# First stage of an encoder layer: an earlier norm, another order of VectorE work and of projection units

## The chip, the cores and the metric

The kernel runs on one core of one Trainium2 chip. The metric is the device time of one execution in microseconds, the median of several runs of the same program. The core has a matrix engine (TensorE, PE in the profile; its weight loads are PEld), VectorE (DVE), ScalarE (ACT), GpSimd (POOL) and a queue of DMA issues (SP). Each engine takes its own instructions in program order and waits on semaphores for the others.

## The reference, cut to what matters

One layer over 1040 tokens (16 meta tokens and 1024 others) of width 1024, all in float32:

```
h = rmsnorm(x)
q, k, v, z, b, a, sc_b, sc_c, sc_x, gate_a, gate_b = split(h @ w_in)
o  = bidirectional chunked gated DeltaNet(silu(conv5(q, k, v)), b, a)     # 8 heads of 128
o  = rmsnorm(o) * silu(z)
ya = o @ w_branch_dn
yb = (sc_b * conv3(sc_c * sc_x)) @ w_branch_sc
x += (sigmoid(gate_a) * ya + sigmoid(gate_b) * yb) @ w_out
x += (silu(gate) * up) @ w_down,  gate, up = split(rmsnorm(x) @ w_gate_up)
out = rmsnorm(x)
```

Inside a head, per chunk of keys k and queries q with decay `exp(g_i - g_j)`: the triangular matrix `I + beta * (k k^T) * decay` is inverted, and a scan over chunks carries a 128x128 state S, forwards and backwards. The change touches the order in which these pieces are issued, not what is computed.

## The kernel before

The kernel has three stages: the projections together with the DeltaNet heads (the first stage, up to about 1060 us), then the branch projections, the merge and the output projection, then the gated feed-forward. Every large product is made as three products of split operands (high times high, high times low, low times high).

**Units.** The first stage is a list of units of projection work, each one column block of 128 of `w_in`. A unit is run by `dense_steps` (L333, matmuls at L340), 24 matmuls for each of its blocks of 320 to 512 tokens, which go into one of two PSUM banks (tag "m"). There are 24 units for q, k and v of the 8 heads (`u_qkv`, L374), 24 units of the short convolution branch (`u_short`, L421: C, X and B for each of 8 column blocks), 16 gate units (`u_gate`, L454) and 5 units of z (`u_z`, L463; the other three z blocks open the second stage, L1395). `pick` (L956) takes the next q, k or v unit when `qkv_ok` allows it and otherwise the first of `fill_units`, whose order before the change is: 24 short convolution units, 16 gate units, 5 z-units. `pick` also starts the load of the unit's weights on SP (L966), one unit ahead; `split_part` (L969) splits them into high and low halves, on ScalarE (L976) and VectorE (L973).

**What the units leave.** A q, k or v chunk is copied by ScalarE into a row buffer `ra` (two of them, `row_buffer`, L347) and convolved on VectorE over two halves (`conv_job`, L355; operations at L362 and L370). A short convolution unit fills a row buffer from C and X (L433, L436), `short_job` (L406; L410, L415) convolves it, B is multiplied in (L450), and the product is stored to `p_d` in device memory (L452). A gate unit is a tanh on ScalarE and a store (L459, L461). A z-unit is a tanh, a VectorE multiplication and a store (L473, L477, L479). The second stage begins with the last three z blocks, then loads all eight `p_d` (L1409) and splits them into `px` (tag "b", L100 and L101), on which the first branch product (L133 to L135) runs.

**Streams.** Beside the units, four streams work for the heads, each one head at a time: `g_decay` (L532) loads and masks the decay matrix PQ (mask at L540, exponential at L545), `g_norm` (L549) makes the chunk products, `g_inv` (L637) the inverse, `g_scan` (L769) the scan. They are Python generators that issue a few instructions and yield the time at which they want to go on. After every projection matmul, `run_streams` (L998) steps each stream that is due, in the order scan, inverse, norm, decay, and `pump` (L316) fills VectorE from three lanes of small jobs: convolutions ("conv"), the forward substitution of the inverse ("fs", L495 and L499) and small norms.

**The planner's clock.** The order is written out by hand, that is, no instruction is moved afterwards (`manual_schedule`). A model of the time stands behind it: `T` holds a time in ns for each engine, `pe(ns)`, `V(n, kind)` and `A(n)` (L265 to L277) advance it by the price of an instruction and return when its result is seen elsewhere. `pump` works while VectorE's modelled time is at most 700 ns ahead of PE's.

**The norm.** `g_norm` transposes k and q into PSUM (`tok`, banks of tag "e", three of them, L575 and its neighbours), takes squares on ScalarE (L563), and then loops over 8 chunks. `kkq(c)` (L602) multiplies a chunk's k with k and q into an "e" bank; two L625 operations make NP, one L629 operation makes PQ, both on VectorE. Before the change `kkq(c + 2)` is issued right after the L629 of chunk c, and the loop yields after the L625 pair and after L629, so other VectorE jobs get in between. `g_inv` begins with four VectorE transposes (L653) and ends with L764 and L765.

**What starts when.** `start_streams` (L979) starts a norm for head h when its convolutions are done and `h < done + 2`. `done` counts scans that have ended wholly, with their output norm (L912 to L920), transposes and stores (L935, L937); `freed` is raised inside the last of a scan's eight steps (L901), after its last L887 product. `g_decay` goes by `freed` already. In a scan step, L850 and L853 multiply the state, L860 forms the right side on VectorE, L866 applies the inverse, L883 and L887 follow, and L896 makes the new state on VectorE. NP has two buffers, and the scan of head h writes its output into NP of head h.

Of the kernel before, what the change touches and what calls it, by code (L numbers as in the profile page):

```python
# [8 lines left out]
F32 = mybir.dt.float32  # L9
# [7 lines left out]
P = 128  # L17
# [7 lines left out]
H = 8  # L25
# [22 lines left out]
def encoder_layer(ctx: ExitStack, tc: tile.TileContext, x, meta, norm1_w, w_in, w_ba,  # L48
# [15 lines left out]
    def uid(s):  # L64
        cnt["n"] += 1
        return f"{s}_{cnt['n']}"
# [198 lines left out]
    def on(e, ns, ready=0.0):  # L265

        T[e] = max(T[e], ready, T["pe"]) + ns
        return T[e] + TOPE
# [5 lines left out]
    def V(n, kind=0):  # L274
        return on("dve", (68 + 1.042 * n, 130 + 1.042 * n, 130 + 0.52 * n)[kind])
# [187 lines left out]
    def u_z(h, w):  # L463

        rest = None
        for i in range(2):
            po = psm()
            for k, _ in enumerate(dense_steps(po, w, hx, META + 512 * i, 512)):
                if k == 11 and rest:
                    rest()  # L470
                yield
            th = half_buffer()[:, :512]
            nc.scalar.activation(th, po, AF.Tanh, scale=0.5)  # L473
            A(512)

            def rest(i=i, th=th, po=po):
                nc.vector.scalar_tensor_tensor(out=th, in0=th, scalar=1.0, in1=po, op0=ALU.add, op1=ALU.mult)  # L477
                V(512)
                nc.sync.dma_start(z_d[h][:, 512 * i:512 * i + 512], th)  # L479
        T["dve"] = max(T["dve"], T["act"] + HOP)  # L480
        rest()
# [67 lines left out]
    def g_norm(h, st_):  # L549

        kq = st_["kq"]
        kT, qT = kq[:, 0], kq[:, 1]
        small = dn.tile([P, 9, 12], F32, tag="small", name=uid("small"), bufs=2)
        st_["small"] = small
        ssk, ssq, rk2, ssk1, y, tmp, sk = (small[:, :, i] for i in range(7))
        cc, ce = small[:, :, 7:9], small[:, :, 9:11]
# [43 lines left out]
        def kkq(c):  # L600
            pk = psd()
            mm(pk[:, :2 * P].rearrange("p (a t) -> p a t", a=2), kT[:, cs(c)], kq[:, :, cs(c)],  # L602
                                  start=True, stop=True)
            return pk, pe(435)

        nxt = [kkq(0), kkq(1)]
        yield T["act"] + HOP
        nc.vector.tensor_scalar(out=ssk1, in0=ssk, scalar1=EPS, scalar2=None, op0=ALU.add)
        nc.vector.reciprocal(rk2, ssk1)
# [2 lines left out]
        nc.vector.tensor_tensor(out=cc, in0=hb, in1=rk2.unsqueeze(2).broadcast_to([P, 9, 2]), op=ALU.mult)  # L612
        nc.vector.tensor_scalar(out=Nm, in0=Nm, scalar1=cc[:META, 8, 0:1], scalar2=None, op0=ALU.mult)
        on("dve", 500)
        NP = dn.tile([P, NC, 2, P], F32, tag="NP", name=uid("NP"), bufs=2)
        PQ = st_["PQ"]
        st_["NP"] = NP
        yield T["act"] + HOP - 300
        for c in range(NC):
            pk, t = nxt.pop(0)  # L620
            while c not in st_["exp"]:
                yield T["pe"] + 200
            yield max(t, st_["exp"][c])
            for d in range(2):
                nc.vector.scalar_tensor_tensor(out=NP[:, c, d], in0=pk[:, 0:P], scalar=cc[:, c, d:d + 1],  # L625
                                               in1=PQ[:, c, d], op0=ALU.mult, op1=ALU.mult)
                V(P, 1)
            yield T["dve"] - 200
            nc.vector.tensor_tensor(out=PQ[:, c], in0=pk[:, P:2 * P].unsqueeze(1).broadcast_to([P, 2, P]), in1=PQ[:, c],  # L629
                                    op=ALU.mult)  # L630
            V(2 * P)
            if c + 2 < NC:
                nxt.append(kkq(c + 2))
            yield T["dve"] - 200
        enqueue("norm", norm_job(st_, ssk1, cc, ce, he, y, tmp, sk))

    def g_inv(h, st_):  # L637
# [14 lines left out]
        for b in range(4):  # L652
            nc.vector.transpose(NP[B(b), :, 1, B(b)], NP[B(b), :, 1, B(b)])  # L653
            on("dve", 467)
            nc.sync.dma_start(nd[b].rearrange("c d j i -> j (c d) i"),
                                             NP[B(b), :, :, B(b)].rearrange("j c d i -> j (c d) i"))
            if b < 3:
                yield T["dve"] - 200
        nc.gpsimd.memset(fP, 0.0)
        nc.gpsimd.memset(fPf[0:64, 0:8 * 33:33], 1.0)  # L660
        nc.gpsimd.memset(fPf[0:64, 8 * 32 + 24:512:33], 1.0)
# [107 lines left out]
    def g_scan(h, st_):  # L769
# [159 lines left out]
        for c4 in range(2):  # L929
            oT = NP[:, 4 * c4:4 * c4 + 4, 1 - c4]  # L930
            pt = newbank()
            for c in range(4):
# [10 lines left out]
                 for h in range(H) for i, off in enumerate((OK, OQ, OV))]  # L943
    fill_units = [(off + j * P, lambda w, j=j, i=i: u_short(j, i, w), None, i)
                  for j in range(8) for i, off in enumerate((OSC, OSX, OSB))]
    fill_units += [(off + j * P, lambda w, j=j, d_=d_[j]: u_gate(j, d_, w), None, None)
                   for j in range(8) for off, d_ in ((OGA, ta_d), (OGB, tb_d))]
    fill_units += [(OZ + h * P, lambda w, h=h: u_z(h, w), None, None) for h in range(ZH)]
    done = freed = 0
    decs, norms, invs, scans = [], [], [], []  # L950

# [27 lines left out]
    def start_streams():  # L979
        nonlocal ndec, nnorm, ninv, nscan  # L980
        h = ndec
        if h < H and h < freed + 2 and not decs:
            decs.append([g_decay(h, heads[h]), T["dve"] + HOP, h])
            ndec += 1
        h = nnorm
        if h < H and h < ndec and h < done + 2 and not norms and all(k in heads[h] and heads[h][k]() for k in ("tk", "tq")):
            norms.append([g_norm(h, heads[h]), T["dve"] + HOP, h])
            nnorm += 1
        h = ninv
        if h < H and not invs and heads[h].get("normed"):  # L990
            invs.append([g_inv(h, heads[h]), T["dve"] + HOP, h])
            ninv += 1
        h = nscan
        if h < H and not scans and heads[h].get("inverted") and "tv" in heads[h] and heads[h]["tv"]():
            scans.append([g_scan(h, heads[h]), T["dve"] + HOP, h])
            nscan += 1
# [809 lines left out]
```

## Time and profile before

| | us |
|---|---|
| median of 3 runs (2005.18 to 2007.22) | 2005.81 |
| the profiled execution | 2006.06 |
| its span, first to last instruction | 2004.3 |
| PE busy in the span | 1985.3 (99%) |
| weight loads busy | 1730.0 (86%) |
| VectorE busy | 1334.7 (67%) |
| ScalarE busy | 816.9 (41%) |
| GpSimd busy | 116.5 (6%) |

In all rows of the profile, "<-" reads "waits for" in a list of waits and "out <- in" in a list of instructions; "x3" is a count; "idle before" is time in which the engine did nothing ahead of an instruction. Times in a timeline count from the first instruction of the span. A matmul's length is modelled and overlaps the next one; the distance between two starts is its cost. VectorE and ScalarE rows that follow each other overlap a little in the same way.

### The profile page before, as it was taken

The page shows a single profiled execution, that of the slowest core. Times are in us where ns is not written, and L with a number is a line of the kernel's source. Part 1 is how long each engine was busy: PE and PEld are TensorE (multiplying, and loading weights), DVE is VectorE, ACT ScalarE, POOL GpSimd, SP SyncE. Part 2 cuts the span into 40 slices and gives each one's busy share as a digit, 9 for nine tenths or more (in the row PEclk, how much of TensorE's full clock was granted, in tenths as well). Part 3 has the DMA queues.
Part 4 walks back from the last instruction along what each step waited for, and adds up shares of the span by engine and source line. Part 5 has one row for each costly group of instructions (what it writes and reads, how often), then busy time and mean ns, then how long its engine had stood idle before and what let it go on. Part 6 is the DMA issues. An engine that isn't in the chain of part 4 may idle for free.

```text
span 2004.3 us, 31913 instructions
## 1 busy us (share of the span) xinstructions
PE 1985.3 (99%) x12059; PEld 1730.0 (86%) x12059; DVE 1334.7 (67%) x2966; ACT 816.9 (41%) x1945; POOL 116.5 (6%) x407
## 2 busy tenths in 40 slices
PE   9999999999999999999999999999999999999998
PEld 8999999999899989888888888887878888888887
DVE  6888677879688878673325434468866666646575
ACT  6471353466255555543324111224423333334344
POOL 2002201002010202010000000000000000000000
PEclk9999999999999999999999999999999999999999
DMA  3121231302212231323237543123666345487654
GB/s 137 61 80 59 64 96 48 96 24 89 75 59 64 69 89 55 106 64 101 79 111 246 205 137 105 63 85 110 248 216 222 139 149 188 158 272 243 195 172 168
DMA packets 131409, 247.85 MB, mean 124 GB/s; under 512 B 45045, under 2 KB 54694, under 8 KB 128823
## 3 DMA queue, kind: packets, MB, share of 16 engines
q1 hardware_dynamic: 130679, 244.77, 36.9%
q8 instruction: 94, 1.54, 0.3%
q10 hardware_dynamic: 576, 1.05, 0.1%
q14 instruction: 60, 0.49, 0.1%
HBM read 179.10 MB, written 66.67 MB: 123 GB/s over the span
## 4 chain that ended last, share of the span: by engine, by line
PE 68%; DVE 5%; DMA 1%; ACT 1%; issue 1%; SPq 0%; DVEq 0%; ACTq 0%
PE pm L340 19%; PE pd L1546 10%; PE pe L1546 4%; PE pm L1546 3%; PE pe L133 1%; PE pe L134 1%; PE pe L135 1%; PE pd L133 1%; PE pd L135 1%; PE pd L134 1%; PE pe L1713 1%; PE pe L1712 1%; PE pe L1714 1%; PE pd L1713 1%; PE pd L1712 1%; PE pd L1714 1%
## 5 line engine op out<-in xcount | busy, mean ns | idle before, releaser
L340 PE MATMUL pm<-al,wh 128*128 128x512 f32 (+4 forms) x1424 | 495.9, 353 | 0.0
L340 PE MATMUL pm<-hTh,wh 128*128 128x512 f32 (+4 forms) x1424 | 495.0, 352 | 0.4 <-ACT hTh L1086 0.2
L340 PE MATMUL pm<-hTh,wl 128*128 128x512 f32 (+4 forms) x1424 | 495.1, 352 | 0.0
L340 PEld LDWEIGHTS pm<-al,wh 128*128 128x128 f32 x1424 | 266.9, 188 | 18.1 <-issue 1.1
L340 PEld LDWEIGHTS pm<-hTh,wh 128*128 128x128 f32 x1424 | 266.8, 188 | 18.0 <-ACT hTh L1086 0.8
L340 PEld LDWEIGHTS pm<-hTh,wl 128*128 128x128 f32 x1424 | 266.9, 188 | 16.7 <-issue 0.4
L973 DVE TENSOR_TENSOR wl<-raw,wh 128x512 fp32r<-128x512 f32 x134 | 90.4, 688 | 64.5 <-ACT wh L976 64.0
L101 DVE TENSOR_TENSOR al<-raw,ring_h 128x1024 fp32r<-128x1024 f32 x73 | 88.7, 1222 | 65.4 <-ACT ring_h L100 64.9
L100 ACT CAST ring_h<-raw 128x1024 fp32r<-128x1024 f32 x73 | 76.7, 1053 | 106.9 <-PE pe L1714 37.2
L362 DVE SCALAR_TENSOR_TENSOR kq<-ra,wc,kq 128x520 f32<-128x520 f32 x128 | 96.9, 757 | 5.8 <-ACT kq L392 4.3
L976 ACT CAST wh<-raw 128x512 fp32r<-128x512 f32 x134 | 79.1, 621 | 13.3 <-PE pm L340 9.6
L100 ACT CAST wh<-raw 128x1024 fp32r<-128x1024 f32 x43 | 45.1, 1050 | 87.8 <-PE pe L134 34.8
L495 DVE TENSOR_TENSOR tm<-fP,fN 128x135 f32<-128x135 f32 (+23 forms) x248 | 72.7, 293 | 6.6 <-DMA fN<-nd 2.5
L499 DVE TENSOR_TENSOR fP<-fP,tm 128x135 f32<-128x135 f32 (+23 forms) x248 | 71.6, 289 | 4.4
L873 ACT ACTIVATE w<-pd,small 128x128 f32<-128x128 f32 x128 | 39.9, 364 | 82.6 <-PE pd L866 75.3
L1649 ACT ACTIVATE b<-b 128x512 f32<-128x512 f32 x22 | 13.9, 632 | 115.4 <-DVE b L1548 115.4
L1548 DVE TENSOR_TENSOR b<-pd,b 128x512 f32<-128x512 f32 x22 | 15.2, 690 | 67.6 <-PE pd L1546 67.6
L101 DVE TENSOR_TENSOR wl<-raw,wh 128x1024 fp32r<-128x1024 f32 x43 | 52.4, 1219 | 11.6 <-ACT wh L100 11.4
L1546 PE MATMUL pd<-b_hl,wh 128*128 128x512 f32 x176 | 54.4, 390 | 0.0
L860 DVE SCALAR_TENSOR_TENSOR r<-pd,negEG,vS 128x128 f32<-128x128 f32 x120 | 36.7, 345 | 26.5 <-PE pd L850 26.5
L545 ACT ACTIVATE PQ<-PQ,negG 128x128 f32<-128x128 f32 x128 | 43.4, 395 | 24.3 <-DVE PQ L540 24.1
L840 ACT ACTIVATE jk<-NP 128x128 f32<-128x128 f32 x64 | 19.9, 311 | 81.8 <-DVE NP L836 80.8
(523 smaller groups left out, 4422.8 us busy)
## 6 DMA issues: line engine op xcount, KB each, us to landing
raw<-in_w_in_dram SPq DMA_DIRECT2D x72, 512.0 KB
raw<-in_w_gate_up_dram SPq DMA_DIRECT2D x44, 512.0 KB
sums<-in_w_down_dram SPq DMA_DIRECT2D x22, 512.0 KB
t_d<-sums SPq DMA_DIRECT2D x11, 1024.0 KB
raw<-s_d SPq DMA_DIRECT2D x44, 256.0 KB
raw<-t_d SPq DMA_DIRECT2D x44, 256.0 KB
act_d<-b SPq DMA_DIRECT2D x43, 256.0 KB
raw<-act_d SPq DMA_DIRECT2D x33, 256.0 KB
```

The source lines that it names most:

```text
L100: nc.scalar.copy(hi, src)
L101: nc.vector.tensor_tensor(out=lo, in0=src, in1=hi.bitcast(F32), op=ALU.subtract)
L133: mm(po[:m, :n], wh[:, k, :m], xhk[:, t0:t0 + n], start=(k == 0), stop=False)
L134: mm(po[:m, :n], wh[:, k, :m], xlk[:, t0:t0 + n], start=False, stop=False)
L340: mm(po[:, :n], ww[:, k], f(k)[:, t0:t0 + n], start=i == 0, stop=i == 3 * KT - 1)
L362: nc.vector.scalar_tensor_tensor(out=acc, in0=raw[:, h0 + t:h0 + t + hn], scalar=wc[:, t, col:col + 1], in1=acc, op0=ALU.mult, op1=ALU.add)
L495: nc.vector.tensor_tensor(out=tv, in0=fP[:, 0:r, j:j + 1].broadcast_to([P, r, n]), in1=fN[:, j:j + 1, j + 1:32].broadcast_to([P, r, n]), o ...
L499: nc.vector.tensor_tensor(out=fP[:, 0:r, j + 1:32], in0=fP[:, 0:r, j + 1:32], in1=tv, op=ALU.subtract)
L545: nc.scalar.activation(PQ[:, c, d], PQ[:, c, d], AF.Exp, bias=negG2[:, c, hd:hd + 1])
L973: nc.vector.tensor_tensor(out=u[1][1][:, k], in0=u[2][:, k], in1=u[1][0][:, k].bitcast(F32), op=ALU.subtract)
L976: nc.scalar.copy(u[1][0][:, k], u[2][:, k])
L1546: mm(po, x[:, k], y, start=k + i == 0 and not add_to, stop=k == 3 and i == 2, skip_group_check=add_to)
```

## The change

A norm may start when `h < freed + 2`. It holds before it takes its NP buffer until `h <= done + 1`. Since a norm can now begin while the scan two heads back still uses its `small` tile, `small` has three buffers instead of two.

In the loop over chunks, `ask()` issues `kkq` when the model says that the bank it will use is free (`freed_at`) and fewer than two are waiting. The two L625 and the L629 of a chunk are issued together, and the loop goes on when PE's modelled time is within 800 ns of the end of what VectorE has been given. As `pump` stops at 700 ns, lanes get little in between. The yield between the first transposes of `g_inv` goes from 200 ns to 800 ns ahead of VectorE.

`fill_units` is turned round: gate units, z-units, and the 24 short convolution units at the end.

```diff
--- before.py
+++ after.py
@@ -550,7 +550,7 @@
 
         kq = st_["kq"]
         kT, qT = kq[:, 0], kq[:, 1]
-        small = dn.tile([P, 9, 12], F32, tag="small", name=uid("small"), bufs=2)
+        small = dn.tile([P, 9, 12], F32, tag="small", name=uid("small"), bufs=3)
         st_["small"] = small
         ssk, ssq, rk2, ssk1, y, tmp, sk = (small[:, :, i] for i in range(7))
         cc, ce = small[:, :, 7:9], small[:, :, 9:11]
@@ -603,7 +603,14 @@
                                   start=True, stop=True)
             return pk, pe(435)
 
-        nxt = [kkq(0), kkq(1)]
+        nxt, freed_at, asked = [kkq(0), kkq(1)], [0.0], 2
+
+        def ask():
+
+            nonlocal asked
+            while asked < NC and asked < len(freed_at) + 2 and freed_at[asked - 2] <= T["pe"]:
+                nxt.append(kkq(asked))
+                asked += 1
         yield T["act"] + HOP
         nc.vector.tensor_scalar(out=ssk1, in0=ssk, scalar1=EPS, scalar2=None, op0=ALU.add)
         nc.vector.reciprocal(rk2, ssk1)
@@ -612,26 +619,33 @@
         nc.vector.tensor_tensor(out=cc, in0=hb, in1=rk2.unsqueeze(2).broadcast_to([P, 9, 2]), op=ALU.mult)
         nc.vector.tensor_scalar(out=Nm, in0=Nm, scalar1=cc[:META, 8, 0:1], scalar2=None, op0=ALU.mult)
         on("dve", 500)
+        while h > done + 1:
+            yield T["pe"] + 100
         NP = dn.tile([P, NC, 2, P], F32, tag="NP", name=uid("NP"), bufs=2)
         PQ = st_["PQ"]
         st_["NP"] = NP
         yield T["act"] + HOP - 300
+        freed_at[0] = T["act"] + HOP
         for c in range(NC):
+            while not nxt or c not in st_["exp"]:
+                ask()
+                yield T["pe"] + 100
             pk, t = nxt.pop(0)
-            while c not in st_["exp"]:
-                yield T["pe"] + 200
-            yield max(t, st_["exp"][c])
+            while T["pe"] < max(t, st_["exp"][c]):
+                ask()
+                yield T["pe"] + 100
             for d in range(2):
                 nc.vector.scalar_tensor_tensor(out=NP[:, c, d], in0=pk[:, 0:P], scalar=cc[:, c, d:d + 1],
                                                in1=PQ[:, c, d], op0=ALU.mult, op1=ALU.mult)
                 V(P, 1)
-            yield T["dve"] - 200
             nc.vector.tensor_tensor(out=PQ[:, c], in0=pk[:, P:2 * P].unsqueeze(1).broadcast_to([P, 2, P]), in1=PQ[:, c],
                                     op=ALU.mult)
-            V(2 * P)
-            if c + 2 < NC:
-                nxt.append(kkq(c + 2))
-            yield T["dve"] - 200
+            freed_at.append(V(2 * P))
+            ask()
+            ready = T["dve"] - 800
+            while T["pe"] < ready:
+                yield T["pe"] + 100
+                ask()
         enqueue("norm", norm_job(st_, ssk1, cc, ce, he, y, tmp, sk))
 
     def g_inv(h, st_):
@@ -655,7 +669,7 @@
             nc.sync.dma_start(nd[b].rearrange("c d j i -> j (c d) i"),
                                              NP[B(b), :, :, B(b)].rearrange("j c d i -> j (c d) i"))
             if b < 3:
-                yield T["dve"] - 200
+                yield T["dve"] - 800
         nc.gpsimd.memset(fP, 0.0)
         nc.gpsimd.memset(fPf[0:64, 0:8 * 33:33], 1.0)
         nc.gpsimd.memset(fPf[0:64, 8 * 32 + 24:512:33], 1.0)
@@ -946,6 +960,7 @@
     fill_units += [(off + j * P, lambda w, j=j, d_=d_[j]: u_gate(j, d_, w), None, None)
                    for j in range(8) for off, d_ in ((OGA, ta_d), (OGB, tb_d))]
     fill_units += [(OZ + h * P, lambda w, h=h: u_z(h, w), None, None) for h in range(ZH)]
+    fill_units = fill_units[24:] + fill_units[:24]
     done = freed = 0
     decs, norms, invs, scans = [], [], [], []
 
@@ -983,7 +998,7 @@
             decs.append([g_decay(h, heads[h]), T["dve"] + HOP, h])
             ndec += 1
         h = nnorm
-        if h < H and h < ndec and h < done + 2 and not norms and all(k in heads[h] and heads[h][k]() for k in ("tk", "tq")):
+        if h < H and h < ndec and h < freed + 2 and not norms and all(k in heads[h] and heads[h][k]() for k in ("tk", "tq")):
             norms.append([g_norm(h, heads[h]), T["dve"] + HOP, h])
             nnorm += 1
         h = ninv
```

## The prediction

> **What bounds the kernel now.** I read the windows first, five of 200 us over the first stage and one behind it. Their columns are length, busy time of PE, weight loads (PEld), DVE, ACT and POOL, then granted clock, DMA share and GB/s.
>
> ```profile
> 50.00:250.00 200.00, 199.84 (x1433) 189.29 (x1432) 161.29 (x399) 86.42 (x269) 26.28 (x99) 1.00 0.21 66
> 250.00:450.00 200.00, 199.40 (x1694) 188.40 (x1693) 158.65 (x457) 103.42 (x341) 14.08 (x61) 1.00 0.22 66
> 450.00:650.00 200.00, 199.24 (x1647) 186.23 (x1647) 163.01 (x483) 94.30 (x311) 27.02 (x91) 1.00 0.23 71
> 650.00:850.00 200.00, 199.02 (x1591) 178.94 (x1590) 155.00 (x469) 107.69 (x345) 28.33 (x90) 1.00 0.26 79
> 850.00:1050.00 200.00, 199.88 (x1243) 168.16 (x1242) 85.64 (x276) 69.32 (x191) 8.95 (x32) 1.00 0.28 87
> 1050.00:1250.00 200.00, 200.00 (x884) 165.60 (x883) 92.28 (x100) 48.89 (x52) 0.00 (x0) 1.00 0.53 177
> ```
>
> In the five rows of the first stage PE idles 0.16 + 0.60 + 0.76 + 0.98 + 0.12 = 2.62 us of 1000. VectorE, the engine that the change reorders, is 78 to 82% busy up to 850 us and 43% behind it. The clock is full in every row. So the order can only be worth what PE waits, unless the order changes what PE's work itself costs. That second point I read from PE's timeline: the scan of the last head between projection matmuls.
>
> ```profile
> 941.10 0.40 PE L340 MATMUL pm<-al,wh 128*128 128x512 f32 x1
> 941.33 0.60 PE L866 MATMUL pd<-r,NP 128*128 128x128 f32 x4
> ...
> 942.01 0.39 PE L340 MATMUL pm<-hTh,wh 128*128 128x512 f32 x1
> 942.24 0.39 PE L340 MATMUL pm<-al,wh 128*128 128x512 f32 x1
> ...
> 944.77 0.40 PE L340 MATMUL pm<-hTh,wl 128*128 128x512 f32 x1
> 945.00 0.61 PE L850 MATMUL pd<-S,kq 128*128 128x128 f32 x4
> 945.45 0.61 PE L853 MATMUL pd<-S,kq 128*128 128x128 f32 x4
> ...
> 946.13 0.40 PE L340 MATMUL pm<-al,wh 128*128 128x512 f32 x1
> ```
>
> The second column (0.40) is a matmul's modelled length; the work is the distance of starts, 942.24 − 942.01 = 0.23 for a projection matmul. One small group costs 942.01 − 941.10 − 2 × 0.23 = 0.45 us. Two groups side by side cost 946.13 − 944.77 − 2 × 0.23 = 0.90, which is twice 0.45. Going in and out of a group is thus not charged extra, and whichever step stands between whichever projection matmuls, the sum is the same. A reordering moves this work and removes none.
>
> [...]
>
> What PE waits for in the first stage (35 to 1050 us; total, times, longest), first the matmuls' own rows and then those of their weight loads:
>
> ```profile
> PE pd L850 <- DVE S L896: 0.8, 2, 0.6
> PE pe L602 <- DVE PQ L629: 0.7, 1, 0.7
> PE pd L754 <- DVE XT L746: 0.4, 1, 0.4
> ...
> PEld pd L850 <- DVE S L896: 2.6, 6, 0.9
> ...
> PEld pe L602 <- PE pm L340: 1.1, 1, 1.1
> ...
> PEld pe L602 <- PE pd L97: 0.3, 1, 0.3
> ```
>
> Lateness of VectorE in the loads' rows is 2.6 at the scan's states and 1.1 + 0.3 at the norm's products; with the 0.4 of L754 it makes 4.4 us. These are the terms that this change can reach.
>
> **The change part by part. 1, asking for kkq only when its bank is free.** The 0.7 looks like this on PE and on VectorE:
>
> ```profile
> 503.91 0.40 PE L340 MATMUL pm<-hTh,wl 128*128 128x512 f32 x1
> 505.01 0.67 PE L602 MATMUL pe<-kq 128*128 128x256 f32 x2 [0.71 <-DVE PQ L629]
> ...
> 503.11 0.60 DVE L625 SCALAR_TENSOR_TENSOR NP<-pe,small,PQ 128x128 f32<-128x128 f32 x2
> 503.63 0.24 DVE L499 TENSOR_TENSOR fP<-fP,tm 128x96 f32<-128x96 f32 x1
> 503.79 0.74 DVE L415 SCALAR_TENSOR_TENSOR rb<-ra,cols,rb 128x512 f32<-128x512 f32 x1
> 504.45 0.41 DVE L629 TENSOR_TENSOR PQ<-pe,PQ 128x256 f32<-128x256 f32 x1
> ```
>
> L602 was issued although its PSUM bank waits for L629, and L629 stood behind a short convolution and a step of the inverse (503.63 to 504.45). Every projection matmul queued behind L602 waited too: 1.10 − 0.23 = 0.87 us. The new loop asks by the modelled time at which the bank is free. Bounds: 0 (the model is late by as much as now) and 1.4 (both rows). I take 0.9, the one stall whose rows show it. The number of products stays, and so do the two L625 and one L629 of a chunk.
>
> **2, precedence of the decay loop.** Chunks now follow each other: two L625 take 0.52 from start to start and L629 0.34 (timeline at 639.85 to 640.19 below), so 8 chunks hold VectorE 8 × 0.86 = 6.9 us in which scan operations, convolutions and the inverse get only the gaps.
>
> ```profile
> 636.25 0.69 DVE L765 COPY NP<-pd 64x512 f32<-64x512 f32 x1 [1.84 <-ACT NP L764]
> ...
> 639.85 0.42 DVE L629 TENSOR_TENSOR PQ<-pe,PQ 128x256 f32<-128x256 f32 x1
> 640.19 0.60 DVE L625 SCALAR_TENSOR_TENSOR NP<-pe,small,PQ 128x128 f32<-128x128 f32 x2
> ...
> 646.24 0.42 DVE L653 STREAM_TRANSPOSE NP<-NP 32x256 f32<-32x256 f32 x1
> ```
>
> The planner books these operations, so a scan matmul is placed later and PE runs projections instead: 0, hidden by the projections. Without that cover each chunk that delays a state costs 0.86.
>
> **3, the norm two heads back starts at `freed`, not `done`.** What is skipped is the tail of a scan. For the last head the rows are:
>
> ```profile
> 976.62 0.61 PE L887 MATMUL pd<-v,PQ 128*128 128x128 f32 x4
> ...
> 984.99 1.26 ACT L935 COPY NP<-pd 128x512 f32<-128x512 f32 x2 [4.60 <-PE pd L97]
> ```
>
> That is 986.25 − 976.62 = 9.6 us here. The transposes and squares move into it; the loop waits for `done`, since NP has two buffers. But a head's inverse is one at a time: L765 ends the previous one at 636.94 and L653 begins the next at 646.24. The head gains at most those 9.3 us in this place. What is late next is the inverse, not PE. Earlier heads shorten the stage only if projections run out, and they do not:
>
> ```profile
> 1059.58 0.32 SPq L479 DMA_DIRECT2D z_d<-rb  x1
> 1063.51 7.87 SPq L1409 DMA_DIRECT2D s<-p_d  x5
> 1073.93 2.59 SPq L1409 DMA_DIRECT2D s<-p_d  x3
> ...
> 1084.29 1.22 DVE L101 TENSOR_TENSOR b<-s,b 128x1024 fp32r<-128x1024 f32 x1
> ...
> 1089.31 0.39 PE L133 MATMUL pd<-b,wh 128*128 128x512 f32 x1
> ```
>
> The last z-unit of the stage is stored from 1059.58, so projections run on for some 73 us past the last head's end at 986.25. Worth 0. The third `small` buffer costs no instruction.
>
> **4, short convolutions last.** Their VectorE work up to now lies among the heads:
>
> ```profile
> L415 DVE SCALAR_TENSOR_TENSOR rb<-ra,cols,rb 128x512 f32<-128x512 f32 x32 | 23.9, 745 | 0.3
> L450 DVE TENSOR_TENSOR rb<-pm,rb 128x512 f32<-128x512 f32 x16 | 10.9, 683 | 2.1 <-PE pm L340 2.0
> ```
>
> With the smaller operations of the same units left out these are 34.8 us, part of which moves to where VectorE is 43% busy. Over the four busy rows, 637.95 us of VectorE, that is some 5%, so the lateness at L850 (2.6 us in 6 stalls) shrinks and does not vanish, the more so as heads come closer together. Bounds 0 and 2.6; between ends this far apart I take 1.1, just under the half, since convolutions of q, k and v stay among the heads. Moved with it: 16 stores to p_d, which now come last on SP's queue, past the gates' and z-units' stores. The loads at L1409 follow them. Now the first load waits from 1059.58 to 1063.51 behind a z-store; then it waits behind a p_d store of the same size. The eighth load is issued by 1076.52, 17 us after the last store. Its result is split by 1085.51 and PE wants it 7 × 3 × 0.23 = 4.8 us after 1089.31, so 8.6 us are spare: 0, and only what exceeds 8.6 if that cover is gone.
>
> **5, the inverse's yield of 800 instead of 200.** It puts up to three transposes earlier on VectorE: 0, hidden by the inverse's wait for its DMAs.
>
> **Sum:** 0.9 + 1.1 = 2.0 us. The profiled execution took 2006.06 (span 2004.3, so 1.76 around it), 0.25 above the median of the runs, 2005.81. From it 2004.06, by the median 2003.8; I say 2004.0.
>
> **The rivals.** *All lateness goes:* the 4.4 us, hence 2001.7. For it: all of it is a wait for VectorE; against it: the scan's states stay behind convolutions. *Lateness only moves:* 2006.0, nothing gained, because heads packed closer load VectorE as before; the 78 to 82% in four rows speak for it.
>
> *Slower, by starved convolutions:* each projection chunk of q, k or v is evicted by ScalarE into one of two row buffers, and a buffer is free when VectorE has convolved it. If the norm's 6.9 us fall into such a unit and the convolution is already late, ScalarE stands before the eviction and PE with it when both projection banks are full.
>
> ```profile
> L362 DVE SCALAR_TENSOR_TENSOR kq<-ra,wc,kq 128x520 f32<-128x520 f32 x128 | 96.9, 757 | 5.8 <-ACT kq L392 4.3
> ```
>
> A unit's convolution has 8 such operations, 6.1 us; a unit is 24 matmuls on each of 336, 320 and 384 columns, at 0.23 us for 512 columns 24 × 1040 / 512 × 0.23 = 11.2 us, and a buffer comes round after two units, 22.4 us. It decides once a convolution is more than 22.4 − 6.1 = 16 us late. Price: the norm's whole 6.9 for one head, less the gain of part 1: 2006.06 + 6.9 − 0.9 = 2012. Against it: no row of PE or its loads names a row buffer now.
>
> *The stage boundary:* p_d is late by more than 8.6 us. One store's 3.9 more leaves it hidden; four of them in a row, 15.7, would leave 7.1 open, 2006.06 + 7.1 = 2013. Against it: the stores of a unit are 24 matmuls, 5.5 us, apart, longer than the 3.9. *Heads set the stage after all:* 9.3 us for each of the six heads from the third on, 2006.06 − 55.8 = 1950; against it stand the 73 us of projections behind the last head.
>
> **How the numbers follow.** Forecast 0.45, all lateness gone 0.17, moved 0.17, starved convolutions 0.14, boundary 0.04, heads 0.03. About 0.2%, 4 us, is what a measurement of this kernel can tell from no change: faster means under 2001.8, slower over 2009.8. Faster: most of 0.17, a tail of the forecast and 0.03, together 0.23; slower 0.14 + 0.04 = 0.18; the same 0.59. The forecast's own range is 2002 to 2006. The range for 8 in 10 goes from 2000.0 (below the 2001.7, as a stall's rows may not show all of it) to 2010.0, leaving out the heads' case and most of starved convolutions.
>
> **What would show it.** Right: PE's idle time between 50 and 1050 falls from 2.62 to about 1; L602 no longer waits; L625 and L629 alternate with little between them; L887 ends before 977; L133 on px begins near 1087. Part 4 is wrong if L850 keeps its 2.6. The whole is wrong if projections wait for ScalarE or VectorE (L340 rows), or if L133 waits for px; or if the starts of equal matmuls change their distance.

## The result, and the profile after

| | before | after |
|---|---|---|
| median us | 2006.56 (2005.18 to 2009.43, 21 runs) | 2010.45 (2007.88 to 2012.81, 21 runs) |
| ratio, 95% interval | | 1.0018 [1.0011, 1.0025] |
| profiled execution, its span | 2006.06, 2004.3 | 2009.93, 2008.2 |
| first stage, first to last start of L340 | 1039.7 | 1044.9 |
| PE idle, 50 to 1050 (sum of five rows) | 2.62 | 4.82 |

The change makes the kernel 3.9 us slower; 2 us faster was forecast. The median less the length of the first stage is 966.8 us before and 965.5 after, and between 965.3 and 968.3 for each of the 20 kernels told of here. So the difference lies in the first stage. It can't be read finer than those 3 us allow, as the length is of one execution and the median of many.

In the rows below, the code of before has moved down: L625 is L638 now, L629 L641, L653 L667, L708 L722, L850 L864, L887 L901, L896 L910, L937 L951. The windows of after, with the columns of the prediction:

```profile
50.00:250.00 200.00, 199.71 (x1306) 175.99 (x1305) 153.28 (x394) 93.86 (x284) 26.26 (x92) 1.00 0.26 83
250.00:450.00 200.00, 199.74 (x1622) 179.99 (x1621) 162.45 (x494) 111.35 (x363) 22.66 (x94) 1.00 0.25 78
450.00:650.00 200.00, 199.11 (x1604) 179.28 (x1603) 163.91 (x492) 108.32 (x350) 22.02 (x92) 1.00 0.25 78
650.00:850.00 200.00, 197.44 (x1650) 183.70 (x1650) 162.50 (x489) 97.11 (x327) 25.45 (x91) 0.99 0.23 69
850.00:1050.00 200.00, 199.18 (x1407) 187.31 (x1406) 83.25 (x209) 48.55 (x135) 0.40 (x4) 1.00 0.20 64
```

The first three rows are as before to a few tenths. The fourth lost 1.6 us and the fifth 0.7 us more, and the clock of the fourth is 0.99. What PE and its weight loads wait for (35 to 1050 us; total, times, longest):

```profile
PE pe L602 <- DVE PQ L641: 2.5, 2, 2.4
...
PEld pe L602 <- issue: 4.8, 8, 2.7
...
PEld pd L864 <- DVE S L910: 0.8, 3, 0.4
```

The scan's states, 2.6 us before, are down to 0.8. In place of them one product of the norm waits 2.4 us for a PSUM bank; the 2.7 of its weight loads is the same wait. The timeline of after at that place, PE first, then VectorE:

```profile
681.79 0.34 PE L340 MATMUL pm<-hTh,wl 128*128 128x384 f32 x1
684.51 0.67 PE L602 MATMUL pe<-kq 128*128 128x256 f32 x2 [2.38 <-DVE PQ L641]
...
676.42 0.43 DVE L722 STREAM_TRANSPOSE XT<-NP 32x256 f32<-32x256 f32 x1 [2.53 <-DMA NP<-pd]
677.14 0.43 DVE L723 STREAM_TRANSPOSE XT<-NP 32x256 f32<-32x256 f32 x1 [0.29 <-DMA NP<-pd]
677.76 0.44 DVE L724 STREAM_TRANSPOSE Xe<-NP 32x256 f32<-32x256 f32 x1 [0.19 <-DMA NP<-pd]
679.38 0.69 DVE L988 TENSOR_TENSOR wl<-raw,wh 128x512 fp32r<-128x512 f32 x1 [1.18 <-ACT wh L991]
...
683.31 0.59 DVE L638 SCALAR_TENSOR_TENSOR NP<-pe,small,PQ 128x128 f32<-128x128 f32 x2
683.94 0.42 DVE L641 TENSOR_TENSOR PQ<-pe,PQ 128x256 f32<-128x256 f32 x1
```

Read it from the end. L602 needs the bank that L641 of chunk 0 frees at 684.36. L641 is that late because VectorE stood still 2.53 + 0.29 + 0.19 + 1.18 = 4.2 us, 3.0 of it for a load by which the inverse of another head gets its blocks. From the timeline of SP:

```profile
668.78 0.67 SPq L479 DMA_DIRECT2D z_d<-rb  x1
674.62 1.92 SPq L706 DMA_DIRECT2D NP<-pd  x4
```

By the trace's semaphore updates, which tell of landings, the first of these four loads had landed at 676.40, 1.8 us after its issue. It was issued late: SP stood until the store that it reads back (the last of three of pd<-fP, L701, issued at 667.10) had landed at 674.48, after 7.4 us. The planner allows `LAND` = 5.5 us for it. In the 20 traces told of here, before included, this store took 6.5 to 8.4 us in each of 160 cases. `ask()` goes by the planner's clock, in which these blocks had come in time. What followed is in the windows of 2 us behind the wait:

```profile
682.00:684.00 2.00, 0.13 (x1) 0.00 (x0) 1.79 (x8) 0.00 (x0) 0.00 (x0) 1.00 0.20 33
684.00:686.00 2.00, 1.49 (x95) 1.19 (x98) 1.97 (x6) 0.69 (x2) 0.00 (x0) 0.86 0.58 230
686.00:688.00 2.00, 2.00 (x31) 1.76 (x19) 1.90 (x7) 0.36 (x1) 0.00 (x0) 0.50 0.00 0
688.00:690.00 2.00, 2.00 (x10) 1.77 (x9) 1.51 (x5) 0.68 (x2) 0.00 (x0) 0.78 0.00 0
```

The granted clock falls to 0.50; by the shares it lost 2 × (0.14 + 0.50 + 0.22) = 1.7 us. The wait and the clock together are 2.4 + 1.7 = 4.1 us, about what the kernel lost. Over the kernels below, the change of PE's idle time in the stage and of the lost clock agrees with the change of the median within 2.7 us (for `v3_dummy` with the added work counted); smaller differences can't be read from these sums.

The heads end earlier, as the change means them to (976.62 before for the last product into the output), and the border to the second stage holds, though p_d is stored last. From the timelines of PE, SP and VectorE:

```profile
932.74 0.61 PE L901 MATMUL pd<-v,PQ 128*128 128x128 f32 x4
...
1058.30 5.36 SPq L452 DMA_DIRECT2D p_d<-rb  x2
...
1086.23 1.23 DVE L101 TENSOR_TENSOR b<-s,b 128x1024 fp32r<-128x1024 f32 x1 [2.76 <-ACT b L100]
...
1095.05 0.39 PE L133 MATMUL pd<-b,wh 128*128 128x512 f32 x1
```

The eighth part of px is split at 1087.46 and wanted 4.8 us after 1095.05: 12 us are spare.

### The profile page after: what moved, and what is told of

Read it like the earlier page. It is cut to its first block, busy times and chain, and to the rows that moved or that the text cites. A ratio compares the mean times of both kernels' runs of the same rounds, so it can differ in the third digit from the quotient of the medians.

```text
span 2008.2 us, 31913 instructions
## 1 busy us (share of the span) xinstructions
PE 1988.4 (99%) x12059; PEld 1730.0 (86%) x12059; DVE 1341.5 (67%) x2966; ACT 815.6 (41%) x1945; POOL 108.6 (5%) x407
## 4 chain that ended last, share of the span: by engine, by line
PE 90%; DVE 5%; ACT 2%; DMA 2%; issue 1%; SPq 0%; POOL 0%; DVEq 0%; ACTq 0%; POOLq 0%
PE pm L340 35%; PE pd L1561 11%; PE pe L1561 5%; PE pm L1561 3%; PE pe L133 1%; PE pe L135 1%; PE pe L134 1%; PE pd L901 1%; PE pe L602 1%; PE pd L133 1%; PE pd L135 1%; PE pd L134 1%; PE pd L880 1%; PE pe L1728 1%; PE pe L1727 1%; PE pe L1729 1%
## 5 line engine op out<-in xcount | busy, mean ns | idle before, releaser
L340 PE MATMUL pm<-hTh,wh 128*128 128x512 f32 (+4 forms) x1424 | 496.6, 353 | 0.4 <-ACT hTh L1101 0.2
L340 PE MATMUL pm<-al,wh 128*128 128x512 f32 (+4 forms) x1424 | 495.1, 352 | 0.0
L340 PE MATMUL pm<-hTh,wl 128*128 128x512 f32 (+4 forms) x1424 | 494.5, 352 | 0.0
L340 PEld LDWEIGHTS pm<-hTh,wh 128*128 128x128 f32 x1424 | 267.0, 188 | 18.0 <-ACT hTh L1101 0.8
L340 PEld LDWEIGHTS pm<-hTh,wl 128*128 128x128 f32 x1424 | 267.1, 188 | 17.1 <-issue 0.8
L340 PEld LDWEIGHTS pm<-al,wh 128*128 128x128 f32 x1424 | 267.1, 188 | 16.5 <-issue 0.4
L100 ACT CAST wh<-raw 128x1024 fp32r<-128x1024 f32 x43 | 45.1, 1050 | 99.2 <-PE pe L134 35.3
L887 ACT ACTIVATE w<-pd,small 128x128 f32<-128x128 f32 x128 | 39.9, 364 | 100.7 <-PE pd L880 100.4
L495 DVE TENSOR_TENSOR tm<-fP,fN 128x135 f32<-128x135 f32 (+23 forms) x248 | 71.9, 290 | 4.6 <-DVE fP L499 0.2
```

The source lines that it names most:

```text
L100: nc.scalar.copy(hi, src)
L340: mm(po[:, :n], ww[:, k], f(k)[:, t0:t0 + n], start=i == 0, stop=i == 3 * KT - 1)
L495: nc.vector.tensor_tensor(out=tv, in0=fP[:, 0:r, j:j + 1].broadcast_to([P, r, n]), in1=fN[:, j:j + 1, j + 1:32].broadcast_to([P, r, n]), o ...
```

## The experiments

All runs side by side, each beside runs of before taken with it; "fill" is the turned `fill_units`, "norm" the start at `freed` with the hold and the third `small`, "loop" the new loop over chunks with `ask()` and the 800 ns of the inverse. The last column is the time in the first stage at clock 0.50, in us; after itself has 3.4.

| run | what | ratio to before | stage | PE idle 50 to 1050 | half clock |
|---|---|---|---|---|---|
| u2_no_fill | norm + loop | 1.0003 [0.9994, 1.0012] | 1039.6 | 4.63 | |
| u3_no_norm | fill + loop | 1.0034 [1.0022, 1.0047] | 1046.7 | 6.05 | 3.4 |
| u4_no_loop | fill + norm | 1.0018 [1.0009, 1.0027] | 1042.4 | 4.92 | |
| v4_fill_alone | fill | 0.9990 [0.9981, 0.9999] | 1038.5 | 2.50 | |
| w2_norm_alone | norm | 1.0056 [1.0044, 1.0068] | 1049.7 | 11.77 | 6.8 |
| w3_loop_alone | loop | 1.0037 [1.0025, 1.0049] | 1047.3 | 8.11 | |
| u1_margin | all, asked 3 us later | 0.9999 [0.9990, 1.0007] | 1040.8 | 3.15 | |
| v3_dummy | all, 22 transposes in the wait | 1.0015 [1.0006, 1.0024] | 1043.5 | 2.14 | |
| v1_land_after | all, 4 us more for landings | 1.0049 [1.0037, 1.0062] | 1049.4 | 8.88 | 3.4 |
| w1_land_od | v1, and 5 us more for o_d | 1.0042 [1.0030, 1.0054] | 1047.0 | 7.69 | 3.4 |
| v2_land_before | before, 4 us more for landings | 1.0003 [0.9994, 1.0012] | 1040.5 | 2.86 | |
| w4_fill_land | fill, 4 us more for landings | 0.9998 [0.9989, 1.0006] | 1038.6 | 2.33 | |
| x1_norm_hold | norm, 12 us more if it held | 1.0060 [1.0048, 1.0072] | 1051.4 | 12.36 | 6.8 |
| y1_norm_stored | norm, 12 us after o_d's issue | 1.0005 [0.9996, 1.0014] | 1038.3 | 3.01 | |
| x2_loop_margin | loop, asked 3 us later | 1.0030 [1.0018, 1.0042] | 1044.1 | 5.11 | 3.4 |
| x3_loop_1us | loop, asked 1 us later | 1.0042 [1.0029, 1.0055] | 1048.5 | 7.91 | 3.4 |
| y2_loop_200 | x2, goes on at 200 ns | 1.0019 [1.0010, 1.0028] | 1042.3 | 4.41 | |
| x4_fill_loop_margin | fill + loop, asked 3 us later | 1.0032 [1.0020, 1.0044] | 1044.5 | 6.36 | |

**The wait of L602 itself.** `u1_margin` asks later, all else as after:

```diff
-            freed_at.append(V(2 * P))
+            freed_at.append(V(2 * P) + 3000)
```

> The changed kernel with one edit: in the norm's loop a PSUM bank counts as free 3000 ns later than modelled, so that TensorE gets a chunk's product (L602) later in its own order. Late-bank theory: in the changed kernel's profile TensorE stood 2.38 us before one L602 because VectorE, which had waited 2.53 us for the DMA of the inverse, freed the bank later than the planner's clock had it, and the clock was then granted at 0.50 for some 2 us; together 4 to 4.5 us. Then the margin brings 2006 (ratio to the kernel before 0.999 to 1.0005), no wait of L602 over 0.5 us, and a mean clock back at 0.999. Order-of-units theory (the cost lies in the short convolutions at the end of the stage): the margin changes nothing, ratio about 1.0018, clock 0.997.

Measured 2006.11 us, 4.3 less than after, and the row of L602 is gone from PE's waits:

```profile
PE pd L747 <- ACT T L741: 0.9, 1, 0.9
PE pd L864 <- DVE S L910: 0.8, 2, 0.5
```

So the stall of L602 is what the change loses by as it stands. The margin also spreads the chunks of the norm, and no run parts the two here. With the stall gone the kernel is as fast as before, not 2 us faster: its largest rows are now the two above, one of the inverse and one of the scan. `v3_dummy` leaves the order alone and adds 22 transposes of the identity, into a bank that nothing reads, ahead of the product that waits (`if h == 6 and asked == 3` in `ask()`), so that PE is busy in that place:

> The changed kernel with 22 transposes of the identity (0.11 us each, 2.4 us, nothing reads them) put in front of the one L602 that stood 2.38 us. The matrix engine works instead of waiting, VectorE's lateness stays. If the lost clock is a cost of its own: no granted 0.50 near 685 us, 1.7 us less than the changed kernel, ratio about 1.001 against its 1.0018. If the clock does not matter, or the idle time does not cause it: the same time as the changed kernel, 1.0018, or slower by up to 2.4 us where the wait is shorter in a run.

The stage is 1.4 us shorter than after and no half clock is left in it (granted 1.00 in each of the five windows from 50 to 1050 us), so with PE busy there the clock did not fall. The 1.4 is of one execution each; the medians, 2010.45 and 2009.41, point the same way, but their ratios' intervals overlap, so the price of the clock rests on its granted share.

**The parts two by two.** Each leaves one part of the change out.

> The changed kernel with the old order of units (short convolutions first); early norm and new loop stay. Order-of-units theory: back to the kernel before, ratio 1.000. Late-bank theory: the stall sits where an inverse's DMA wait meets the norm's loop, which the order of units shifts only by chance: a stall of 1 to 3 us at some L602 remains likely (ratio 1.0005 to 1.002), and whatever the ratio, TensorE's waits plus the lost clock account for it within 1 us.

> The changed kernel with the norm starting at done, as before (small with two buffers); new loop and new order of units stay. Late-bank theory: without the early start the loop comes some 20 us later, behind the DMA wait of the other head's inverse, so that the L602 stall goes, ratio 0.999 to 1.0005. Theory that the new loop's hold on VectorE costs by itself: ratio stays near 1.0018 with L864 or L340 rows waiting.

> The changed kernel with the old loop over chunks (L602 issued right behind the L629 before it, 200 ns yields); early norm and new order of units stay. Late-bank theory: the old loop is late too when VectorE's clock is wrong, L602 is issued with no look at the bank, so a stall can be as long or longer: ratio 1.0005 to 1.003. Theory that the new loop's hold on VectorE is the cost: ratio at or below 1.000.

No part carries the loss: without `fill` it is gone, without `norm` it nearly doubles, without `loop` it stays, by another wait. In `u4_no_loop` this is a state of the scan, late behind an inverse's step (VectorE, then PE):

```profile
614.99 0.25 DVE L495 TENSOR_TENSOR tm<-fP,fN 128x31 f32<-128x31 f32 x1 [5.12 <-POOL tm L679]
...
616.25 0.59 DVE L898 SCALAR_TENSOR_TENSOR S<-S,eGl,pd 128x128 f32<-128x128 f32 x2
...
616.63 0.74 PE L852 MATMUL pd<-S,kq 128*128 128x128 f32 x4 [2.35 <-DVE S L898]
```

VectorE takes its own queue in order (in the trace of before all its 2966 instructions stand in the program's order): L898 stood behind an L495 that waited 5.12 us. The row names GpSimd's L679, but L495 reads none of its results; it reads fN, whose last load was issued at 609.41 and landed at 614.77. So here too a transfer of the inverse was late.

**More time for landings.** `LAND` in the inverse goes from 5500 to 9500 and two `yield T["pe"] + 5600` to 9600, on three kernels: after, before, and fill alone.

> The changed kernel with the planner's three allowances for the inverse's DMAs raised by 4000 ns (LAND 5500 to 9500, two waits of 5600 to 9600), nothing else. Landing theory: VectorE's waits for those DMAs (11.5 us at L722 in the changed kernel) are the source of its lateness, so they fall under 4 us, no L602 or L864 stalls over 1 us, the clock stays at 1.00 inside the first stage, and the time is 2005.5 to 2006.5 (ratio 0.9985 against the changed kernel's 1.0018, that is 0.9995 to 1.0005). Theory that only the asking by modelled time in the norm's loop is at fault: the DMA waits shrink, but stalls at L602 stay, ratio 1.001 to 1.002. A stage bound by its heads would get slower, by 8 us for a pair of heads.

> The kernel before with the same raised allowances. Landing theory: its own lateness rows at the scan (2.6 us of loads at L850) and the 15.4 us of VectorE at L708 shrink too; gain of up to 3 us, ratio 0.9985 to 1.000. If the kernel before has no such source of lateness: 1.000, and its L850 rows stay.

> A candidate for the best: the new order of units alone (2004.6 in v4) with the allowances up by 4000 ns, norm and loop as before. Landing theory: VectorE's 12.1 us at L708 go and with them the stalls of 1.2 and 1.1 us: 2002.5 to 2004.5, ratio 0.998 to 0.999. If v4's remaining stalls have another source: 2004.6 as in v4.

On after it does harm, against the landing theory. VectorE's wait for the inverse's loads falls (L722: 11.5 to 2.1 us), and another row comes up; behind it, in the timeline, one of its places:

```profile
DVE NP L638 <- DMA o_d<-NP: 7.5, 3, 3.8
```

```profile
390.75 0.61 DVE L638 SCALAR_TENSOR_TENSOR NP<-pe,small,PQ 128x128 f32<-128x128 f32 x2 [2.76 <-DMA o_d<-NP]
```

The first L638 of a head writes into the NP from which the head two back is still being stored to o_d. `done` says only that this store was issued. On before and on fill alone there was nothing to gain, though VectorE's waits at L708 went. On before the last scan now ends 42 us later (1019.2 against 977.2), and the time is the same. `w1_land_od` lets a norm that held go on 5 us later on top of `v1_land_after`:

```diff
+        held = h > done + 1
         while h > done + 1:
             yield T["pe"] + 100
+        if held:
+            yield T["pe"] + 5000
```

> The kernel of v1 (changed kernel, allowances up by 4000 ns; 2016.8) with one more wait in the plan: a norm that had to hold for done goes on 5000 ns later, so that the store of o_d from the same NP buffer has landed. Landing theory: v1's waits of VectorE at L638 for that store (7.5 us, 3 times) and with them its L602 stalls (2.55, 1.5, 1.5 us) and the half clock at 620 us go; time 2004.5 to 2006.5, ratio 0.999 to 1.000. Theory that the new loop itself causes the L602 stalls: they stay, ratio over 1.002.

A miss: 7.1 us of that wait remain.

**One part alone.** `v4_fill_alone` turns `fill_units` and nothing else.

> The kernel before with the new order of units alone (short convolutions last). Order-of-units theory, from three variants with this order at 2010 to 2013 and the one without it at 2006.6: slow by itself, ratio 1.002 or more. Landing theory without a part for the order: the stalls fall by chance, ratio between 1.000 and 1.002, and TensorE's waits in the first stage plus lost clock account for the difference within 1 us. My forecast of before: 0.9995.

It had 2004.59 us (2003.12 to 2006.44, 11 runs) beside 2006.59 and has the lowest ratio of all. Its loads wait less for the states, 2.6 us before:

```profile
PEld pd L850 <- DVE S L896: 1.5, 2, 1.3
```

But PE idles as long as before (2.50), so it isn't shown that the 2.0 us come from there. `w4_fill_land`, with the same order, had 0.9998; the intervals of the two overlap.

`w2_norm_alone` and `w3_loop_alone`:

> The kernel before with the early norm alone (start at freed, hold before NP, third small buffer). Landing theory: the old norm's transposes and squares lay between done and the first write to NP and so hid the landing of o_d; started early they hide nothing, and VectorE's first L625 waits for the store (2 to 4 us) in some heads; with the old loop L602 goes out unasked and waits; ratio 1.000 to 1.003, DMA o_d rows at L625. If the early start is harmless: 1.000 and no such row.

> The kernel before with the new loop alone (asking by modelled time, a chunk's three operations together, yields of 800). Landing theory: no new DMA stands before the loop, so ratio 0.999 to 1.0007, L602 waits under 1 us. Theory that the loop's hold on VectorE is the cost: ratio 1.001 to 1.003, with waits at L852 or L340.

Both cost more than expected. The norm alone, from the timelines of SP, VectorE and PE, and a window of 4 us:

```profile
688.83 0.38 SPq L939 DMA_DIRECT2D o_d<-NP  x1
689.31 1.62 SPq L689 DMA_DIRECT2D pd<-fP  x3
...
691.70 0.38 SPq L939 DMA_DIRECT2D o_d<-NP  x1
...
698.60 0.61 DVE L627 SCALAR_TENSOR_TENSOR NP<-pe,small,PQ 128x128 f32<-128x128 f32 x2 [8.21 <-DMA o_d<-NP]
...
699.82 1.19 PE L602 MATMUL pe<-kq 128*128 128x256 f32 x2 [7.00 <-DVE PQ L631]
```

```profile
694.00:698.00 4.00, 0.00 (x0) 0.00 (x0) 0.00 (x0) 0.00 (x0) 0.15 (x1) 0.79 0.19 60
```

The store of the second half was issued at 691.70; L627 may write when it has landed, 6.9 us later, and for 4 us no engine but GpSimd does anything. A norm that starts at `done` spends that time on transposes and squares. Such a store does not always take so long. The first half, issued at 688.83, had landed at 691.12, after 2.3 us. Between the two stand the inverse's pd<-fP stores. In the 20 traces, 83 stores to o_d were issued while a pd<-fP store was on its way and took 6.3 us (median); the other 237 took 2.5. That the one holds up the other is argued from this, not tested.

**Is the store all of it?** `x1_norm_hold` is norm alone with the edit of `w1_land_od` at 12000 ns.

> Norm alone (w2: ratio 1.0056, PE idle 11.77 us in 50 to 1050), and a norm that had to hold for its NP buffer goes on 12 us after the planner's `done`, so the o_d store of the head two back has landed before L627 writes into that buffer. Theory (the early norm's whole cost is the store that the planner's clock does not hold): the wait of L627 for the DMA of o_d falls from 12.2 us to under 1, the wait of L602 for L631 from 9.4 to under 1.5, PE idle to 2.5 to 4, ratio 0.999 to 1.001. Rival (transposes, squares and third tile among the scan's steps cost by themselves): the DMA wait goes, but the ratio stays above 1.003 with waits at the scan's states.

Another miss. The row of o_d fell from two waits to one, but at the longest the edit did not act: the norm reached this place just after `done`, so it had not held, and L630 waited as long as before:

```profile
590.82 0.39 SPq L942 DMA_DIRECT2D o_d<-NP  x1
...
597.73 0.61 DVE L630 SCALAR_TENSOR_TENSOR NP<-pe,small,PQ 128x128 f32<-128x128 f32 x2 [8.18 <-DMA o_d<-NP]
```

`y1_norm_stored` counts from the issue of the store, whoever comes first:

```diff
-        while h > done + 1:
+        while h > done + 1 or T["pe"] < stored + 12000:
...
             nc.sync.dma_start(o_d[h][:, c4 * 512:(c4 + 1) * 512].rearrange("p (c t) -> p c t", c=4), oT)
+            stored = T["pe"]
```

> The hold of 12 us did not act in the run before: the norm came to its NP buffer just after `done`, was not held, and L630 waited 8.2 us for o_d, issued at 590.82. Here the norm alone goes on only 12 us of the planner's time after the last o_d was issued, whoever came first. Theory (the store is the whole cost of an early norm): the wait of VectorE for o_d's DMA is under 0.5 us, L602 under 1.5, no half clock within the stage, PE idle 2.5 to 4.5, ratio 0.999 to 1.001. Rival (the early transposes and squares cost by themselves): the wait goes, the ratio stays above 1.003.

The row of o_d is gone, L602 waits little, and the ratio is 1.0005:

```profile
PE pe L602 <- DVE PQ L631: 0.7, 2, 0.6
PE pd L852 <- DVE S L898: 0.6, 2, 0.3
```

The store in front of the reused buffer is thus all that could be measured of the early norm's cost; nor is anything gained by starting it early (its loop can't, with this hold).

**What does the loop cost?** PE's waits with the loop alone:

```profile
PE pe L602 <- DVE PQ L639: 4.5, 4, 1.6
PE pm L340 <- DVE rb L450: 1.3, 1, 1.3
```

Late transfers are not all of it: ahead of two of the four L602 waits (1.6 at 155.73 us and 0.9 at 508.39) VectorE has no wait for a transfer in the 30 us before, and none over 0.2 us for anything in the last 8. There it was busy, later than the planner had it. The cause is either the asking or the hold on VectorE. Two runs ask later, by 3 us and by 1 us:

> Loop alone (w3: ratio 1.0037, stage 1047.3, PE idle 8.11), and kkq is asked 3 us after the time at which the model has its bank free. Theory (asked too early: the new loop issues kkq at the modelled end of the L639 three chunks back, where the old one issued it a chunk later): L602 waits fall from 4.5 us to under 0.5, PE idle to 2.5 to 4, ratio 0.999 to 1.001. Rival (the loop holds VectorE, and convolutions, L450, the inverse and the scan come late behind it): L450, L766 and L817 rows stay, ratio 1.002 to 1.004. The margin also spreads the chunks, so a gain is for asking only together with the run with 1 us.

> As the one before, but with 1 us of margin, about a chunk's 0.86 us, which hardly spreads the chunks. Theory (asked too early): the four L602 waits (longest 1.6) lose up to 1 us each, 4.5 falls to 1 to 1.5, PE idle to 4 to 5.5, ratio 1.000 to 1.0025. Rival (hold of VectorE): the L602 row shrinks as well, but the other rows take its place, PE idle 7 to 9, ratio 1.003 to 1.0045.

The 3 us take the L602 row away and about a fifth of the loss, the 1 us nothing, as far as three ratios with overlapping intervals tell (1.0037, 1.0030, 1.0042). L450 remains, and in both runs its wait is followed by a half clock that the loop alone does not have (1.7 us of the loss); in the run with 3 us (VectorE, then PE), and below it, before:

```profile
167.25 0.42 DVE L639 TENSOR_TENSOR PQ<-pe,PQ 128x256 f32<-128x256 f32 x1
...
168.50 1.54 DVE L415 SCALAR_TENSOR_TENSOR rb<-ra,cols,rb 128x512 f32<-128x512 f32 x2
...
172.00 0.68 DVE L450 TENSOR_TENSOR rb<-pm,rb 128x512 f32<-128x512 f32 x1
...
172.83 0.39 PE L340 MATMUL pm<-hTh,wh 128*128 128x322 f32 x1 [1.85 <-DVE rb L450]
```

```profile
165.38 0.73 DVE L415 SCALAR_TENSOR_TENSOR rb<-ra,cols,rb 128x512 f32<-128x512 f32 x1
...
166.05 0.67 DVE L450 TENSOR_TENSOR rb<-pm,rb 128x512 f32<-128x512 f32 x1
...
170.79 0.68 DVE L450 TENSOR_TENSOR rb<-pm,rb 128x512 f32<-128x512 f32 x1
```

L450 is VectorE's reading of a projection bank. The short convolution that it needs ran among the norm's chunks before and runs behind them now, so the bank stays full until 172.68 and PE stands. `y2_loop_200` has the same margin and lets lanes in between chunks again (`ready = T["dve"] - 200`):

> Loop alone with 3 us of margin (ratio 1.003, stage 1044.1, L340 waiting 1.8 us for L450, which stood behind the loop and behind short convolutions that the loop had put back, and then 3.4 us at half clock), with `ready` at 200 ns instead of 800 ns ahead of VectorE's end, so that the lanes get work between the chunks as in the kernel before. Theory (what is left is the hold on VectorE): no L450 wait above 0.3, no half clock at 174, PE idle 2.5 to 4, ratio 0.999 to 1.001. Rival (any other order of the norm costs): ratio above 1.002 with other rows.

L450 no longer waits, there is no half clock, and the ratio is 1.0019: half the loss of the loop alone. So by the rows the hold costs as well as the asking; the ratios' intervals overlap from each step to the next. What is left, some 3.5 us, stands in part in rows of 1 us each that no run took apart (the first is of the inverse, whose 800 ns are still in):

```profile
PE pd L766 <- DVE XT L758: 1.2, 2, 1.0
PE pm L340 <- DVE wl L985: 1.1, 1, 1.1
PE pd L862 <- DVE S L908: 1.1, 2, 0.8
```

`x4_fill_loop_margin` joins the fill and the loop with 3 us:

> Short convolutions last and the new loop with 3 us of margin, old norm start: what is left of the change without the early norm and with late asking. Theory (asking and unlanded transfers are all that costs): part 4's gain is kept, ratio 0.998 to 1.000, stage 1037 to 1040, and L602 waits under 0.5; the waits behind the inverse's transfers (DVE L720, 22.2 us in the run of fill and loop) remain on VectorE. Rival (the hold costs): above 1.001. It could be the fastest of all; short convolutions last alone had 0.999.

A miss for the theory: L602 waits no more, but the ratio is that of `u3_no_norm` without the margin. Its longest waits are 2.0 us of PE for L815 (VectorE, scan) and 1.4 us for L739 (ScalarE, inverse). Why the same margin sets the loss to nothing beside the early norm and to no avail without it stays open.

## Why the prediction was wrong

**What held.** Projections set the stage, not the heads: the last scan ends 44 us earlier and nothing is gained, and in `v2_land_before` it ends 42 us later and nothing is lost. A reordering is worth what PE waits, and the clock with it, within the 2.7 us told above; that PE's work is the same in any order is not shown more closely than that. The border kept its cover. Part 4, −1.1 with a bound of 2.6, measured −2.0 alone (0.9990, [0.9981, 0.9999]): right in sign and within its bounds, though PE's idle time does not show it.

**Part 1 failed first**, "the new loop asks by the modelled time at which the bank is free", −0.9 with bounds 0 and 1.4. No loss was allowed, because a model "late by as much as now" was taken for the worst. But the old loop asked only once the next chunk had been issued. That this slack covered VectorE's waits for loads is argued, not tested; before has 15.4 us of them at L708 and one wait of L602, 0.7 us. The new loop has no slack, and the model does not hold these waits: 2.4 us in one place, and 1.7 us of clock. The stall of 0.71 at 505 us was read rightly, as VectorE had no wait for a load in the 50 us ahead of it, and it is gone from after. But what it was to bring did not come either: with the margin, where the new stall is gone too, the kernel has 0.9999. There the waits only moved, a rival that was given 0.17.

**Part 2**, "0, hidden by the projections", was right only for what the planner books in PE's order. The loop alone costs 0.37%, and in part by the mechanism of the rival of starved convolutions, though not at its place: not row buffers of q, k and v behind ScalarE, but a projection bank that VectorE empties for a short convolution. In the changed kernel part 4 has moved these units out of its way, and no row of PE there names a row buffer. That this rival had the nearest time (2012 beside 2010.45) is luck: what the changed kernel loses, it loses at L602.

**Part 3**, "the loop waits for `done`, since NP has two buffers", took `done` for the end of the tail. It is the issue of the store; landing took 6.9 us more at the longest waits of two runs. Alone the early norm costs 0.56%. In the changed kernel no row names o_d, so there part 3 cost nothing in the event.

**The sum failed as a sum.** By medians against their own runs of before, the parts alone cost −2.0 (fill), +11.3 (norm) and +7.8 us (loop), and together 3.9. They are not terms to add: each order has its own few places in which PE's hand-written order meets a VectorE that is later than the planner has it. Part 5 was not run by itself.

**"The clock is full in every row"** was read as a property of the stage. In after it was 0.50 for 3.4 us behind the wait of 2.4 us; the sum had no term for it, and it cost 1.7 us.

## What to carry to other kernels

In a program whose order is written out by a model of time, look up for each edit which waits the model does not hold (landings of loads, and stores out of a buffer that is written again), and what slack covered them so far: an order that is tighter by the model takes that slack away. A flag that says "issued" is no flag for "free". An allowance that the trace shows to be too short is not yet a loss: 4 us more for the inverse's landings gained nothing in any of three kernels. The one edit that gained here, by 0.1%, only shifts work away from a busy engine, with no tighter handover.

## What was not expected of the hardware

This is about the granted clock. In the trace of after its record begins with these pieces (start in us, length, granted share):

```
 13.02  672.43  1.0
685.45    3.41  0.5
688.86  706.56  1.0
```

All pieces start on one grid, here 13.02 + n × 3.4133 us: 685.45 is n = 197, 688.86 n = 198. In the trace of before the grid starts at 12.08, and the slow piece at 1391.06 is n = 404. The wait of after, from 682.13 to 684.51, lies in one field of the grid, 682.03 to 685.45. That of `u4_no_loop`, as long (614.28 to 616.63), has the line at 615.44 in its middle, and the clock stayed full (1.00 in the windows from 612 to 620). Counted over all fields from 50 to 1055 us in the traces of the 20 kernels: ten fields had PE idle for 1.79 us or more, and the field behind each ran at 0.50; the others had 1.38 us or less, and none was followed by a slower one. Near 1390 us, in the second stage, PE stands in every kernel, and there too 1.99 to 2.92 us in a field were followed by 0.50, while 1.71 us (before, field from 1384.24) were not. By its share each field at 0.50 lost 1.7 us (half of 3.41). That PE's idle time within one field decides is read from these counts: no run moved a wait against the grid, and what sets the grid is not shown.
